# Additions and SiLUs of a gate/up block in a two-layer decoder trunk: placed in the program by hand instead of by a planner

## The chip, the cores and the metric

The kernel runs on one core of one Trainium2 chip. The metric is the device time of one execution in microseconds (us). The time before is the median of three runs. A profile comes from one further execution, which has its own time. TensorE (PE) does the matrix products and loads their weights (PEld), VectorE (DVE) and ScalarE (ACT) do elementwise work, GpSimd (POOL) almost none, and SyncE (SP) issues the loads.

## The reference, cut to what matters

The trunk has one Mamba-2 layer and one attention layer on 256 tokens of width 2048, each followed by a SwiGLU network of width 5632:

```
h = h + mamba2_mixer(rmsnorm(h, ...), ...)
h = h + swiglu(rmsnorm(h, ffn_norm_w[0]), w_gate_up[0], w_down[0])
k, v, cum = shared_kv(h, ...)
h = h + forgetting_attention(rmsnorm(h, ...), k, v, cum, ...)
h = h + swiglu(rmsnorm(h, ffn_norm_w[1]), w_gate_up[1], w_down[1])

def swiglu(h, w_gate_up, w_down):
    g, u = jnp.split(h @ w_gate_up, 2, axis=-1)
    return (jax.nn.silu(g) * u) @ w_down
```

The change touches only the product with `w_gate_up` and the `silu(g) * u` behind it, in both layers.

## The kernel before, in words

All weights are float32. Each weight tile is split into a rounded part `whi` (a cast on ACT, L246) and a remainder `wlo` (a subtraction on DVE, L252), and the activations likewise. A product is then three matmuls of 128x128 by 512 columns: high by high (L491), high by low (L492), low by high (L493). `stream` walks through a list of pieces, each of two 128-row weight slices. It splits a piece some steps (`SPL` = 4) before the piece's matmuls are issued, into rings of four `whi` and four `wlo` buffers, and it issues the loads (L333, 1 MB each, a ring of `RAW` = 3 buffers) behind the splits that free them.

In the gate/up product (`ffn_up`, L616) one block is 512 columns of the gate (left) and 512 of the up half (right), for both tiles of 128 tokens. There are 11 blocks in each layer, 22 in all. The first three quarters of the inner dimension are done plainly: six loads, twelve pieces of 12 matmuls. These accumulate in four PSUM banks of the pool `acc`: left[0], left[1], right[0], right[1]. The last quarter is done in seven products instead of eight, out of sums of the operands (a Strassen-Winograd scheme): the class `Cross`, whose steps run in the order d g a c e b f, six matmuls each (L409 to L411). `split_cross` (L357) splits the operand of each step and forms sums of weights by DVE additions at L364. The products g, b and f are added onto left[0], left[1] and right[0] in PSUM. The product a gets right[1], whose content ACT first copies away (`rest`, L390). The products d, c and e get banks of the pool `mis`.

The steps behind the seven products are those of `early`, `first`, `second` and `third`, generators (tasks) that are put into a queue by `cross_step` behind the steps g, e, b and f:

- `early`: ACT copies d out (L626), DVE forms sg = g + d (L621), ACT applies the gate's SiLU to it (L629). This frees left[0].
- `first`: DVE forms v = e - v and y = c - v (L621).
- `second`: DVE forms y = y + b (L621), which frees left[1]; then ACT applies the SiLU to y (L642).
- `third`: four more additions (L621), two multiplications by the SiLUs (L656), and the transposes of the result on TensorE (L527).

The next block starts with its piece n0, whose six matmuls for token tile 0 go to left[0] and whose next six go to left[1] (before the down projection, where the two alternate by three, the same banks follow). Its pieces are called n0, n1, ... below.

Every engine works through its instructions in the order of the program. Where the tasks' instructions stand in that order is decided by a planner, `Flow`. It keeps a clock for each engine (`at`: E for TensorE, A, V), adds estimated costs to them (1.3 for six matmuls, 1.14 or 1.22 for the subtraction of a split, 0.66 for an addition), and `pump`, called after each six matmuls, issues the next part of the first task in the queue if the task's time and the clocks of A and V are at most 4.0 ahead of E. When a product has its matmuls issued, E is first raised to the planned end of that product's split. When a block's first matmuls are about to be issued, the task of the block before last is finished up to its `EVAC` mark:

```
held.append(b)
if len(held) > 2:
    flow.finish(held.popleft().task, evac=True)
```

Of the kernel before, what the change touches and what calls it, by code (L numbers as in the profile page):

```python
# [38 lines left out]
SPL = 4  # L39
# [45 lines left out]
class Task:  # L85


    def __init__(self, gen, queue, ready=0.0):
        self.gen, self.queue, self.ready = gen, queue, ready
        self.done, self.evac, self.sync, self.on, self.last = False, False, False, None, "E"  # L90


class Flow:
# [7 lines left out]
    def spawn(self, gen, queue=None):  # L101
        q = self.urgent if queue is None else queue
        t = Task(gen, q, max(self.at["E"], self.current.ready if self.current else 0.0))
        q.append(t)
        return t
# [84 lines left out]
class Cross:  # L190
# [6 lines left out]

    ORDER = "dgacebf"

    def __init__(self, left, right, units, x, tasks):  # L200
        self.left, self.right, self.units, self.x, self.tasks = left, right, units, x, tasks
        self.ps, self.rest = {}, None


# [1 line left out]
def kernel(ctx: ExitStack, tc: tile.TileContext, xT_d, x_d, cols_d, rows_d, wdt_d, win_d,  # L206
# [27 lines left out]
    def tok(name):  # L234
        return work.tile([P, NB], F32, tag="tok", name=nm(name))
# [67 lines left out]
        b.units.append(Unit(b, 0, src, width, [list(range(a, min(a + step, nk))) for a in range(0, nk, step)]))  # L303
        blocks.append(b)

    def pair(xs, src_l, src_r, tasks, fills):


        both = []
        for src in (src_l, src_r):  # L310
            b = Block(xs, None, fills if src is src_r else None)
            b.paired = True
            if src is src_r:
                b.stops[1] -= KT
            for kg in range(len(xs) - 1):
                b.units.append(Unit(b, kg, src[kg].rearrange("p (k n) -> p k n", n=NB), NB, [[0, 1], [2, 3]]))
            blocks.append(b)
            both.append(b)
        last = [Unit(None, len(xs) - 1, src[len(xs) - 1].rearrange("p (k n) -> p k n", n=NB), NB, [list(range(KT))])
                for src in (src_l, src_r)]  # L320
        blocks.append(Cross(*both, last, xs[-1], tasks))

    def slot_of(s):
        flow.finish(s.task)
# [57 lines left out]
    def cross_step(x, name, parts):  # L382

        hi, lo, ready = parts
        flow.work("E", 0.0, ready)
        s = slot_of(x.x)
        left, right = x.left.ps, x.right.ps
        if name == "d":
            x.rest = phase.tile([P, NB], F32, tag="c4", name=nm("rest"))
            nc.scalar.copy(out=x.rest, in_=right[1])  # L390
            flow.work("A", 0.48)
        own = {"g": left[0], "b": left[1], "f": right[0]}
        if name in own:
            ps = own[name]
        elif name == "a":
            ps = right[1]
        else:
            ps = bank([P, NB])
        x.ps[name] = ps

        def a_of(part, p):
            if name in "dgb":
                k, t = {"d": (1, 0), "g": (0, 0), "b": (0, 1)}[name]
                return s[:, part, 2 * p + k, t * P:(t + 1) * P]
            return x.x.sums[:, "acef".index(name), part, p, :]

        for p in range(2):
            xh, xl = a_of(0, p), a_of(1, p)
            nc.tensor.matmul(ps, lhsT=xh, rhs=hi[:, p, :], start=p == 0 and name not in own, stop=False)  # L409
            nc.tensor.matmul(ps, lhsT=xh, rhs=lo[:, p, :], start=False, stop=False)  # L410
            nc.tensor.matmul(ps, lhsT=xl, rhs=hi[:, p, :], start=False, stop=p == 1)  # L411
        if name in x.tasks:
            task = spawn(x.tasks[name](x))
            if name == "b":
                x.left.task = task
            if name == "f":
                x.right.task = task
                if x.right.fills is not None:
                    x.right.fills.task = task
        flow.work("E", STEP)  # L420
        flow.pump()

    def stream(pre_load, pre_split):
# [30 lines left out]
        split_to(SPL - 1)  # L454
        held = deque()
        for i, (u, ks) in enumerate(pieces):
            split_to(i + SPL)
            if isinstance(u, Cross):
                cross_step(u, ks, parts[i])
                continue  # L460
            b = u.blk
            nk = KT * len(b.xs)
            hi, lo, ready = parts[i]
            flow.work("E", 0.0, ready)
            if u.width < NB:
                if b.ps is None:
                    b.ps = bank([2 * u.width, T])
                for j, k in enumerate(ks):
                    both = hi[:, j].rearrange("p a n -> p (a n)")
                    s = slot_of(b.xs[k // KT])  # L470
                    nc.tensor.matmul(b.ps, lhsT=both, rhs=s[:, 0, k % KT, :], start=k == 0, stop=False)
                    nc.tensor.matmul(b.ps, lhsT=both, rhs=s[:, 1, k % KT, :], start=False, stop=k == nk - 1)
                flow.work("E", 0.22 * len(ks))
                if ks is u.pieces[-1]:
                    b.task = spawn(b.done(b.ps))
                continue
            if b.ps is None:
# [3 lines that stand above are left out]
                b.ps = [acc.tile([P, u.width], F32, tag="acc", name=nm("acc")) for _ in range(NT)]  # L481
            last = u is b.units[-1] and ks is u.pieces[-1]
            order = [(j, t) for j in range(len(ks)) for t in range(NT)]
            if last or (b.paired and u.kg == 0 and ks[0] == 0):
                order = [(j, t) for t in range(NT) for j in range(len(ks))]
            for n, (j, t) in enumerate(order):
                k = u.kg * KT + ks[j]
                s = slot_of(b.xs[k // KT])
                xh = s[:, 0, k % KT, t * P:(t + 1) * P]
                xl = s[:, 1, k % KT, t * P:(t + 1) * P]  # L490
                nc.tensor.matmul(b.ps[t], lhsT=xh, rhs=hi[:, j, :], start=k == 0, stop=False)  # L491
                nc.tensor.matmul(b.ps[t], lhsT=xh, rhs=lo[:, j, :], start=False, stop=False)  # L492
                nc.tensor.matmul(b.ps[t], lhsT=xl, rhs=hi[:, j, :], start=False, stop=k == b.stops[t])  # L493
                if n % 2 == 1:
                    flow.work("E", STEP)
                    flow.pump()
            if last and not b.paired:
                b.task = spawn(b.done(b.ps))
                if b.fills is not None:
                    b.fills.task = b.task  # L500
# [115 lines left out]
    def ffn_up(xs, r, gu_d):  # L616
        acts = [Slot() for _ in range(NFB)]
        add, sub = ALU.add, ALU.subtract

        def tt(out, in0, in1, op):  # L620
            nc.vector.tensor_tensor(out=out, in0=in0, in1=in1, op=op)  # L621
            return V(0.66)

        def early(x):
            m, d, g = x.ps, tok("d"), tok("sg")
            nc.scalar.copy(out=d, in_=m["d"])  # L626
            yield A(0.48)
            yield tt(g, m["g"], d, add)
            nc.scalar.activation(g, g, AF.Silu, scale=r[0][:, 0:1])  # L629
            yield A(0.6, SILU)  # L630
            x.v, x.g = d, g

        def first(x):
            m, v = x.ps, x.v
            yield tt(v, m["e"], v, sub)
            x.y = tok("y")
            yield tt(x.y, m["c"], v, sub)

        def second(x):
            yield tt(x.y, x.y, x.ps["b"], add)  # L640
            yield EVAC
            nc.scalar.activation(x.y, x.y, AF.Silu, scale=r[0][:, 1:2])  # L642
            yield A(0.6, SILU)

        def third(nb):
            def run(x):
                m, w = x.ps, x.v
                yield tt(w, w, m["a"], add)
                u = tok("u")
                yield tt(u, w, m["c"], sub)  # L650
                yield tt(w, w, m["f"], add)
                yield EVAC
                yield tt(u, u, x.rest, add)
                s = [w, u]
                for t, g in enumerate((x.g, x.y)):
                    nc.vector.scalar_tensor_tensor(out=s[t], in0=s[t], scalar=r[0][:, t:t + 1], in1=g, op0=ALU.mult, op1=ALU.mult)  # L656
                    yield V(0.66)
                yield SYNC
                yield from to_slot(acts[nb], lambda t, f: s[t][:, f * P:(f + 1) * P], None)
            return run  # L660

        for nb in range(NFB):
            pair(xs, gu_d[2 * nb], gu_d[2 * nb + 1], {"g": early, "e": first, "b": second, "f": third(nb)}, acts[nb])
        return acts


# [594 lines left out]
```

## Time and profile before

| | before |
|---|---|
| median of three runs | 2606.91 us (2606.17 to 2607.38) |
| profiled execution, its own time | 2605.81 us |
| its span in the profile | 2604.0 us |
| mean granted TensorE clock | 0.999 of full speed |
| from block to block inside a gate/up stage (transposes at 853.68, 900.11, 946.54 us) | 46.4 us |

The span is the time from the first to the last instruction of the profiled execution; 1.8 us of its time lie around it. Matmul rows overlap: each is shown with 0.39 us although one starts every 0.23 us, so TensorE's gaps are read from the starts. An idle time in brackets names what the instruction waited for.

### The profile page before, as it was taken

What the parts mean: (1) busy time and instruction counts of PE and PEld (TensorE: products, weight loads), DVE (VectorE), ACT (ScalarE), POOL (GpSimd) and SP (SyncE); (2) the same over time, 40 slices, a digit from 0 to 9 for tenths busy, and PEclk for the clock granted to TensorE, in tenths of its full rate; (3) what the DMA queues carried; (4) which work ended last, traced back from release to release, by engine and by line L of the source; (5) the groups of instructions that cost most, each with busy time, mean ns of one, the idle gap of its engine ahead of it and who ended that gap; (6) DMA issues with size and microseconds to landing.
All of it is one profiled execution on the core that took longest, in us unless ns stands there. A gap on an engine that the chain in (4) does not pass through costs nothing.

```text
span 2604.0 us, 29926 instructions
## 1 busy us (share of the span) xinstructions
PE 2541.7 (98%) x11638; PEld 2093.0 (80%) x11638; DVE 1743.0 (67%) x2227; ACT 1326.1 (51%) x1683; POOL 38.4 (1%) x52
## 2 busy tenths in 40 slices
PE   9999999999999999999999999999999999999999
PEld 7888888888877777777888888888877777777887
DVE  6677777654577777777444567775677777776444
ACT  6665565554445454454444556564554544544333
POOL 0000000000000000000000010000000000000000
PEclk9999999999999999999999999999999999999999
DMA  7645455455555545455555555445455554555564
GB/s 273 221 167 178 169 187 184 173 194 189 182 178 186 186 162 200 172 190 183 193 188 188 192 180 195 163 161 179 164 197 188 173 184 162 202 185 180 202 202 144
DMA packets 68319, 481.12 MB, mean 185 GB/s; under 512 B 7600, under 2 KB 8256, under 8 KB 10576
## 3 DMA queue, kind: packets, MB, share of 16 engines
q1 hardware_dynamic: 66672, 468.64, 51.8%
q0 software_dynamic: 1504, 10.57, 1.1%
q8 instruction: 91, 1.49, 0.2%
q14 instruction: 52, 0.43, 0.0%
HBM read 477.00 MB, written 2.18 MB: 184 GB/s over the span
## 4 chain that ended last, share of the span: by engine, by line
PE 92%; DVE 5%; issue 2%; ACT 1%; DMA 0%; SPq 0%; ACTq 0%; DVEq 0%
PE acc L491 27%; PE acc L493 27%; PE acc L492 27%; DVE wlo L252 3%; PE mis L527 1%; DVE y L621 1%; PE mis L912 1%; ACT whi L246 1%; PE acc L410 1%; PE acc L411 1%; PE acc L409 1%; PE mis L411 1%; PE mis L410 1%; PE mis L409 1%; DVE d L621 0%
## 5 line engine op out<-in xcount | busy, mean ns | idle before, releaser
L252 DVE TENSOR_TENSOR wlo<-wraw,whi 128x1024 fp32r<-128x1024 f32 (+1 forms) x851 | 1027.7, 1221 | 622.7 <-ACT whi L246 621.6
L246 ACT CAST whi<-wraw 128x1024 fp32r<-128x1024 f32 (+1 forms) x854 | 883.8, 1049 | 851.4 <-PE acc L493 822.8
L491 PE MATMUL acc<-whi,xT 128*128 128x512 f32 x3040 | 1197.1, 394 | 30.8 <-DVE y L621 30.1
L492 PE MATMUL acc<-wlo,xT 128*128 128x512 f32 x3040 | 1184.9, 390 | 0.8 <-DVE wlo L252 0.8
L493 PE MATMUL acc<-whi,xT 128*128 128x512 f32 x3040 | 1184.6, 390 | 0.0
L491 PEld LDWEIGHTS acc<-whi,xT 128*128 128x128 f32 x3040 | 571.4, 188 | 156.3 <-DVE y L621 39.2
L493 PEld LDWEIGHTS acc<-whi,xT 128*128 128x128 f32 x3040 | 571.1, 188 | 120.0
L492 PEld LDWEIGHTS acc<-wlo,xT 128*128 128x128 f32 x3040 | 571.5, 188 | 117.0 <-DVE wlo L252 1.8
L254 DVE SCALAR_TENSOR_TENSOR wlo<-wraw,cols,whi 128x512 fp32r<-128x512 f32 x192 | 134.6, 748 | 74.3 <-ACT whi L248 73.5
L248 ACT ACTIVATE whi<-wraw,cols 128x512 fp32r<-128x512 f32 x192 | 127.5, 717 | 73.9 <-PE acc L493 68.8
L252 DVE TENSOR_TENSOR xT<-mis,xT 128x512 fp32r<-128x512 f32 x52 | 33.5, 687 | 38.3 <-ACT xT L246 38.3
L246 ACT CAST xT<-mis 128x512 fp32r<-128x512 f32 x52 | 27.9, 589 | 54.5 <-PE mis L527 54.5
L364 DVE TENSOR_TENSOR wraw<-wraw 128x1024 f32<-128x1024 f32 x44 | 53.9, 1226 | 1.5
L364 DVE TENSOR_TENSOR wraw<-wraw,wraw 128x1024 f32<-128x1024 f32 x44 | 53.9, 1224 | 1.5
L410 PE MATMUL acc<-wlo,xT 128*128 128x512 f32 x88 | 37.1, 421 | 16.8 <-DVE wlo L252 16.8
L514 POOL TENSOR_TENSOR rs<-ms,mhalf 128x4 f32<-128x4 f32 (+1 forms) x27 | 29.0, 1075 | 1533.5 <-DVE ms L512 1533.2
L491 PE MATMUL acc<-whi,oT 128*128 128x512 f32 x128 | 50.5, 394 | 0.0
L493 PE MATMUL acc<-whi,oT 128*128 128x512 f32 x128 | 49.9, 390 | 0.0
L492 PE MATMUL acc<-wlo,oT 128*128 128x512 f32 x128 | 49.8, 389 | 0.0
L409 PE MATMUL acc<-whi,xT 128*128 128x512 f32 x88 | 36.9, 419 | 8.9 <-ACT whi L246 8.9
L248 ACT ACTIVATE xT<-mis,cols 128x256 fp32r<-128x256 f32 x64 | 25.5, 475 | 35.1 <-PE mis L527 35.1
L254 DVE SCALAR_TENSOR_TENSOR xT<-mis,cols,xT 128x256 fp32r<-128x256 f32 x64 | 26.8, 478 | 22.3 <-ACT xT L248 22.2
(221 smaller groups left out, 1681.4 us busy)
## 6 DMA issues: line engine op xcount, KB each, us to landing
wraw<-in_gu_dram SPq DMA_DIRECT2D x176, 1024.0 KB, 4.8
wraw<-in_dn_dram SPq DMA_DIRECT2D x88, 1024.0 KB, 4.8
wraw<-in_win_dram SPq DMA_DIRECT2D x78, 1024.0 KB, 4.9
wraw<-in_wout_dram SPq DMA_DIRECT2D x32, 1024.0 KB, 4.8
wraw<-in_wq_dram SPq DMA_DIRECT2D x16, 1024.0 KB, 4.8
wraw<-in_wk_dram SPq DMA_DIRECT2D x16, 1024.0 KB, 4.8
wraw<-in_wv_dram SPq DMA_DIRECT2D x16, 1024.0 KB, 4.8
wraw<-in_wo_dram SPq DMA_DIRECT2D x16, 1024.0 KB, 4.8
```

The lines of the kernel that those rows point to most:

```text
L246: nc.scalar.copy(out=hi, in_=src)
L248: nc.scalar.activation(hi, src, AF.Copy, scale=scal)
L252: nc.vector.tensor_tensor(out=lo, in0=src, in1=hi.bitcast(F32), op=ALU.subtract)
L254: nc.vector.scalar_tensor_tensor(out=lo, in0=src, scalar=scal, in1=hi.bitcast(F32), op0=ALU.mult, op1=ALU.subtract)
L364: nc.vector.tensor_tensor(out=out, in0=in0, in1=in1, op=ALU.add)
L409: nc.tensor.matmul(ps, lhsT=xh, rhs=hi[:, p, :], start=p == 0 and name not in own, stop=False)
L410: nc.tensor.matmul(ps, lhsT=xh, rhs=lo[:, p, :], start=False, stop=False)
L411: nc.tensor.matmul(ps, lhsT=xl, rhs=hi[:, p, :], start=False, stop=p == 1)
L491: nc.tensor.matmul(b.ps[t], lhsT=xh, rhs=hi[:, j, :], start=k == 0, stop=False)
L492: nc.tensor.matmul(b.ps[t], lhsT=xh, rhs=lo[:, j, :], start=False, stop=False)
L493: nc.tensor.matmul(b.ps[t], lhsT=xl, rhs=hi[:, j, :], start=False, stop=k == b.stops[t])
L514: nc.gpsimd.tensor_tensor(out=r, in0=ms, in1=mhalf[:, :width], op=ALU.pow)
```

## The change

The four tasks are replaced by a function `inline`, called by `cross_step` directly behind the matmuls of each step, and one task `rest`, put into the queue behind f. The copy of d stands behind step g, sg = g + d behind step a, v = e - v and y = c - v behind step e, y = y + b behind step b. Both SiLUs move into `rest`, behind its four additions. For step b, `stream` issues the step before the split of the piece four ahead (n1) instead of after it. The left block's task becomes one that is already done, so that the next block forces nothing of the queue.

```diff
-            pair(xs, gu_d[2 * nb], gu_d[2 * nb + 1], {"g": early, "e": first, "b": second, "f": third(nb)}, acts[nb])
+            pair(xs, gu_d[2 * nb], gu_d[2 * nb + 1], inline, rest(nb), acts[nb])
...
@@ cross_step
-        if name in x.tasks:
-            task = spawn(x.tasks[name](x))
-            if name == "b":
-                x.left.task = task
-            if name == "f":
-                x.right.task = task
-                if x.right.fills is not None:
-                    x.right.fills.task = task
+        x.inline(x, name)
+        if name == "b":
+            x.left.task = Task(None, None)
+            x.left.task.done = x.left.task.evac = True
+        if name == "f":
+            x.right.task = x.right.fills.task = spawn(x.rest_of(x))
         flow.work("E", STEP)
         flow.pump()
@@ stream
         for i, (u, ks) in enumerate(pieces):
+            if isinstance(u, Cross) and ks == "b":
+                cross_step(u, ks, parts[i])
+                split_to(i + SPL)
+                continue
             split_to(i + SPL)
             if isinstance(u, Cross):
                 cross_step(u, ks, parts[i])
@@ ffn_up
-        def early(x):
-            m, d, g = x.ps, tok("d"), tok("sg")
-            nc.scalar.copy(out=d, in_=m["d"])
-            yield A(0.48)
-            yield tt(g, m["g"], d, add)
-            nc.scalar.activation(g, g, AF.Silu, scale=r[0][:, 0:1])
-            yield A(0.6, SILU)
-            x.v, x.g = d, g
-
-        def first(x):
-            m, v = x.ps, x.v
-            yield tt(v, m["e"], v, sub)
-            x.y = tok("y")
-            yield tt(x.y, m["c"], v, sub)
-
-        def second(x):
-            yield tt(x.y, x.y, x.ps["b"], add)
-            yield EVAC
-            nc.scalar.activation(x.y, x.y, AF.Silu, scale=r[0][:, 1:2])
-            yield A(0.6, SILU)
-
-        def third(nb):
+        def inline(x, name):
+
+            m = x.ps
+            if name == "g":
+                x.v = tok("d")
+                nc.scalar.copy(out=x.v, in_=m["d"])
+                flow.work("A", 0.48)
+            elif name == "a":
+                x.g = tok("sg")
+                tt(x.g, m["g"], x.v, add)
+                flow.work("V", 0.66)
+            elif name == "e":
+                x.y = tok("y")
+                tt(x.v, m["e"], x.v, sub)
+                tt(x.y, m["c"], x.v, sub)
+                flow.work("V", 1.32)
+            elif name == "b":
+                tt(x.y, x.y, m["b"], add)
+                flow.work("V", 0.66)
+
+        def rest(nb):
             def run(x):
                 m, w = x.ps, x.v
                 yield tt(w, w, m["a"], add)
                 u = tok("u")
                 yield tt(u, w, m["c"], sub)
                 yield tt(w, w, m["f"], add)
                 yield EVAC
                 yield tt(u, u, x.rest, add)
                 s = [w, u]
+                for t, g in enumerate((x.g, x.y)):
+                    nc.scalar.activation(g, g, AF.Silu, scale=r[0][:, t:t + 1])
+                    yield A(0.6, SILU)
                 for t, g in enumerate((x.g, x.y)):
                     nc.vector.scalar_tensor_tensor(out=s[t], in0=s[t], scalar=r[0][:, t:t + 1], in1=g, op0=ALU.mult, op1=ALU.mult)
                     yield V(0.66)
                 yield SYNC
                 yield from to_slot(acts[nb], lambda t, f: s[t][:, f * P:(f + 1) * P], None)
             return run
```

## Rows read from the trace of the kernel before

**Rows 1.** The page's first part: busy time, share of the span, instructions.

```profile
PE 2541.7 (98%) x11638; PEld 2093.0 (80%) x11638; DVE 1743.0 (67%) x2227; ACT 1326.1 (51%) x1683; POOL 38.4 (1%) x52
```

**Rows 2.** Waits of TensorE: who waited for whom, us in total, times, longest.

```profile
PE acc L491 <- DVE y L621: 30.1, 21, 2.1
PE acc L410 <- DVE wlo L252: 16.8, 22, 0.8
PE acc L409 <- ACT whi L246: 8.9, 22, 1.7
```

**Rows 3.** Timeline of one block, TensorE's rows: start, length, [idle before <- releaser].

```profile
919.88 0.39 PE L409 MATMUL mis<-whi,xT 128*128 128x512 f32 x1
...
926.45 0.39 PE L411 MATMUL mis<-whi,xS 128*128 128x512 f32 x1
...
927.18 0.49 PE L409 MATMUL acc<-whi,xT 128*128 128x512 f32 x1 [0.34 <-ACT whi L246]
...
928.44 0.50 PE L410 MATMUL acc<-wlo,xT 128*128 128x512 f32 x1 [0.77 <-DVE wlo L252]
...
932.20 0.39 PE L493 MATMUL acc<-whi,xT 128*128 128x512 f32 x1
...
933.96 0.50 PE L491 MATMUL acc<-whi,xT 128*128 128x512 f32 x1 [1.37 <-DVE y L621]
...
946.38 0.27 PE L527 MATMUL mis<-ident,d 128*128 128x128 f32 x1
```

**Rows 4.** Timeline of the same block, DVE's rows.

```profile
921.21 1.23 DVE L252 TENSOR_TENSOR wlo<-wraw,whi 128x1024 fp32r<-128x1024 f32 x1 [0.24 <-ACT whi L246]
922.47 1.23 DVE L364 TENSOR_TENSOR wraw<-wraw 128x1024 f32<-128x1024 f32 x1
923.61 1.22 DVE L252 TENSOR_TENSOR wlo<-wraw,whi 128x1024 fp32r<-128x1024 f32 x1
924.75 0.68 DVE L621 TENSOR_TENSOR sg<-acc,d 128x512 f32<-128x512 f32 x1
927.16 4.63 DVE L252 TENSOR_TENSOR wlo<-wraw,whi 128x1024 fp32r<-128x1024 f32 x4 [1.73 <-ACT whi L246]
931.71 0.68 DVE L621 TENSOR_TENSOR d<-mis,d 128x512 f32<-128x512 f32 x1
932.42 0.69 DVE L621 TENSOR_TENSOR y<-mis,d 128x512 f32<-128x512 f32 x1
933.22 0.69 DVE L621 TENSOR_TENSOR y<-y,acc 128x512 f32<-128x512 f32 x1
933.82 2.35 DVE L252 TENSOR_TENSOR wlo<-wraw,whi 128x1024 fp32r<-128x1024 f32 x2
...
941.74 0.75 DVE L656 SCALAR_TENSOR_TENSOR u<-u,rs,y 128x512 f32<-128x512 f32 x1
```

**Rows 5.** Timeline of the same block, ACT's rows.

```profile
920.12 1.06 ACT L246 CAST whi<-wraw 128x1024 fp32r<-128x1024 f32 x1 [1.67 <-PE acc L493]
...
922.51 0.58 ACT L626 COPY d<-mis 128x512 f32<-128x512 f32 x1
925.47 0.72 ACT L629 ACTIVATE sg<-sg,rs 128x512 f32<-128x512 f32 x1 [2.38 <-DVE sg L621]
926.10 3.87 ACT L246 CAST whi<-wraw 128x1024 fp32r<-128x1024 f32 x4
931.44 1.99 ACT L246 CAST whi<-wraw 128x1024 fp32r<-128x1024 f32 x2 [1.48 <-DMA wraw<-in_gu_dram]
...
938.47 1.05 ACT L246 CAST whi<-wraw 128x1024 fp32r<-128x1024 f32 x1 [1.70 <-PE acc L493]
```

**Rows 6.** Timeline of the second gate/up stage's first block, ACT's and DVE's rows.

```profile
1886.42 1.28 ACT L629 ACT_TABLE_LOAD   x1 [2.42 <-DVE sg L621]
...
1889.40 4.63 DVE L252 TENSOR_TENSOR wlo<-wraw,whi 128x1024 fp32r<-128x1024 f32 x4 [3.06 <-ACT whi L246]
```

**Rows 7.** The page's DMA issues: count, size, us from issue to landing.

```profile
wraw<-in_gu_dram SPq DMA_DIRECT2D x176, 1024.0 KB, 4.8
```

More of the change, by code (lines that the diff above doesn't have):

```diff
@@ L198, with __init__ @@
     ORDER = "dgacebf"
-    def __init__(self, left, right, units, x, tasks):
-        self.left, self.right, self.units, self.x, self.tasks = left, right, units, x, tasks
+    def __init__(self, left, right, units, x, inline, rest_of):
+        self.left, self.right, self.units, self.x = left, right, units, x
+        self.inline, self.rest_of = inline, rest_of
         self.ps, self.rest = {}, None
@@ L304, in narrow, with pair @@
         blocks.append(b)
-    def pair(xs, src_l, src_r, tasks, fills):
+    def pair(xs, src_l, src_r, inline, rest, fills):
         both = []
@@ L320, in pair @@
                 for src in (src_l, src_r)]
-        blocks.append(Cross(*both, last, xs[-1], tasks))
+        blocks.append(Cross(*both, last, xs[-1], inline, rest))
     def slot_of(s):
```

## The prediction

> **What bounds the kernel now.** I read first the busy shares [rows 1]: TensorE is busy 98% of the span, DVE 67%, ACT 51%. Matmul rows overlap, so this hides gaps, and the second view is TensorE's list of waits [rows 2]. Only three waits come once in each of the 22 gate/up blocks, and all three stand around the seven products: step b's first matmul for its cast, its second for its `wlo`, and a matmul of the next block for the addition of y. Third, I read one block of the timeline, engine by engine.
>
> In TensorE's rows [rows 3] the first five steps d g a c e (30 matmuls, 919.88 to 926.45) run at (926.45 − 919.88)/29 = 0.2266 us each, without a gap. b would follow at 926.68 and starts at 927.18 (0.50 lost); its second matmul would follow at 927.41 and starts at 928.44 (1.03). Then 16 matmuls to 932.20 take 3.76 where 16 × 0.2266 = 3.63 (0.13 of slow restart). The next would start at 932.43, and starts at 933.96 (1.53): it is n0's first matmul into left[1], which y = y + b frees. To the transposes at 946.38 there are 54 matmuls, 12.42 against 12.24 (0.18). Together 0.50 + 1.03 + 0.13 + 1.53 + 0.18 = 3.37 us in each block of 46.4; nothing else in a block stops TensorE.
>
> The cause is in the other two engines' order. ACT [rows 5] copies d out by 923.09 and then has the gate's SiLU next in its queue. That waits 2.38 us for sg = g + d on DVE (924.75 to 925.43), which the program puts behind e's split. The cast of b stands behind the SiLU and starts at 926.10. DVE meanwhile has nothing but `wlo` of b in front and is idle 1.73 us [rows 4]. Then it does four splits in a row (b, f, n0, n1; 1.14 each), and only then v, y and y + b.
>
> **The change part by part.** No instruction is added or taken away; the order changes.
>
> *The SiLU out of ACT's way, sg behind a's step.* Now DVE's queue reads: `wlo` e, `wlo` b, sg, `wlo` f, `wlo` n0, v, y, y + b, `wlo` n1. Up to `wlo` e nothing changes, and its start hangs on TensorE: the cast of c waits for the last piece's buffer (920.12, 0.24 after the cross products start). From there [rows 4, 5]:
> - b's weight sum ends at 922.47 + 1.23 = 923.70. ACT is free since 923.09, and b's ring buffer was g's, read out at about 922.84. ACT's own start behind a DVE end takes 0.04 (925.43 to 925.47), so the cast starts at 923.74, and `wlo` b 1.06 later (as 926.10 to 927.16): 924.80. DVE is ready at 923.61 + 1.14 = 924.75: no idle time is left.
> - sg at 924.80 + 1.14 = 925.94; `wlo` f 0.60 later (as 933.22 to 933.82): 926.54; `wlo` n0 927.68; v 928.82; y 0.71 later, 929.53; y + b 0.80 later, 930.33. TensorE goes on 0.74 after that start (933.22 to 933.96): 931.07 instead of 933.96.
>
> Two parts make this 2.89 us: the idle 1.73, and the split of n1 (1.14), which the new line in `stream` puts behind y + b.
>
> *TensorE on the same clock.* b starts at 926.68; its `wlo` is done at 926.03. f follows at 928.04 and needs `wlo` f at 928.27; it ends at 927.77. n0 follows at 929.40 and needs `wlo` n0 at 929.63; that ends at 928.91. left[0] is free since sg's end at 926.62. n0's second half is due at 930.76 and gets its bank at 931.07. So the first two stalls go, and of the third 0.31 stays, with its restart of 0.18. What is late next is thus the same bank, and DVE's chain from c on sets it. The casts feed this chain in time: f at 924.68, n0 at 925.64 (ACT is free then, and c's buffer since 925.56). Before the down projection the second bank is due 0.68 earlier, but DVE's chain still sets the restart, so the gain there is the same.
>
> *What waits behind the fixed places.* v stands right behind e's matmuls, y + b right behind b's. Were a product late, DVE would stand, and n1's and n2's splits behind it. v comes up at 928.82 while e ends near 926.9, y + b at 930.33 while b ends near 928.3: about 2 us to spare each. `wlo` n1 moves behind y + b, to 930.93 to 932.16; n1 needs it at about 932.8. The cover is 0.7 us; without it each microsecond is TensorE's.
>
> *The SiLUs in `rest`.* They cost 0.72 each as before. By the planner's costs, DVE's clock stands 3 × 1.14 + 3 × 0.66 − 1.3 = 4.1 ahead of TensorE's behind f (splits n0, n1, n2; v, y and y + b; one step), just over the 4.0 allowed, so `rest` starts inside n0: w + a in its middle, the next two additions at its end, the fourth and the first SiLU behind n1, the second SiLU and both multiplications behind n3, the transposes behind n5, one piece later than now. In ACT's queue these SiLUs stand behind casts of n4 and n6 with their operands long there, and ACT waits 1.70 us per piece for TensorE in that stretch [rows 5]: cost nothing; without that cover 1.4 us a block. The last multiplication comes at about 941.4, while the transposes are due near 946.2; now it starts at 941.74 for 946.38 [rows 3, 4].
>
> *Loads.* SP issues as many as before, each behind a split. The load behind f's split goes out at 927.8 instead of 929.5, that behind n1's at 932.2 instead of 931.8. A load lands 4.8 us later [rows 7]: 932.6 and 937.0, for casts that cannot start before about 932.9 and 938.3, when TensorE leaves their buffers at its pace. The load behind e's split keeps its place; its cast was held until 931.44 in this block, and its `wlo` is needed at 935.5, a spare of over 1 us. Cost nothing; if two loads slowed each other by all of a load's length, n2 would wait about 3 us in a block.
>
> *The second stage's first block.* There the SiLU also drags a table load of 1.28 us into the way of b's cast, and DVE idles 3.06 instead of 1.73 [rows 6]. The load moves with the SiLU into ACT's idle time: 1.33 us more, once. The Trainium skill, ScalarE: Activation LUTs (What ACT_TABLE_LOAD costs), counts a drain with the load, about 2.66 us for a switch; by that this block would give about 2.7 us more in place of 1.33 and the sum would grow by 1.3. The row shows the SiLU 0.01 us behind the load's end, so 1.33 stands.
>
> **Sum.** 22 × 2.89 = 63.6, and 1.3: 64.9 us off. The profiled execution's 2605.81 (span 2604.0 and 1.8 around it) becomes 2540.9; the median lies 1.1 above that execution: 2542.0. A difference of 0.2% (5.2 us) is about what a measurement of this kernel can tell from no change. Spacings on DVE can be off by 0.2 us in a chain of nine, 4 to 5 us in all: 2537 to 2548 for this case.
>
> **The rivals.**
> - *The bank wait keeps its length.* b's stalls go, but y + b comes no sooner after n0 than now: only 0.50 + 1.03 + 0.13 = 1.66 a block, 22 × 1.66 + 1.3 = 37.8, 2569. For it: the last bank wait is the longest of the three, and from 921.2 to 934 DVE is idle for those 1.73 us alone. Against it: n1's 1.14 leaves DVE's way by the order of the program alone. A rule of the Trainium skill, Perfetto Trace Analysis (Identifying Performance Opportunities), speaks for it: a gap that repeats can mean too few PSUM buffers, which no reordering mends. The trace agrees in that a bank is what is waited for, but the bank is held by an addition waiting its turn. Chance 8%.
> - *TensorE never stops.* If y + b ends 0.3 sooner than counted, all 3.37 go: 22 × 3.37 + 1.3 = 75.4, 2531.5. Chance 8%.
> - *It does not change what TensorE waits for:* b's cast held by its weight sum, b's `wlo` by sg or by splits. Then 2602 to 2612. It needs b's sum 2.4 us later than 923.70; the row has no such delay. Chance 4%.
> - *Slower: DVE stands at v or y + b.* It decides once the products come more than 2.0 + 2.9 = 4.9 us later than counted against DVE's queue; at 6 us late each block loses 1.1 us, 2607 + 24 = 2631. b's operands are ready 0.6 us ahead of b, so nothing in the rows makes it late. Chance 3%.
>
> My forecast holds 74%; the remaining 3% lie between it and the first rival. The range from 2531 to 2558 takes in the forecast, TensorE that never stops, and DVE chains up to 0.7 us longer per block. Faster by over 0.2%: 93%; within 0.2%: 4%; slower: 3%.
>
> **What would show it.** In the profile after: no wait of step b for cast or `wlo`; TensorE's wait for y's addition down from 1.37 to some 0.2 us as listed; DVE without idle time from `wlo` e to y + b, with sg between the splits of b and f; SiLUs without a wait for DVE; 43.5 us from block to block. I am wrong if a new name stands in TensorE's waits (`wlo` of n1, a transpose, a load), or if the bank wait is still over 1 us.

## The result and the profile after

| | before | after |
|---|---|---|
| median | 2607.14 us (4 runs, 2606.17 to 2610.39) | 2543.02 us (4 runs, 2542.06 to 2543.43) |
| ratio, 95% interval | | 0.9751 [0.9734, 0.9768] |
| span of the profiled execution | 2604.0 us | 2541.7 us |
| from block to block in a gate/up stage | 46.43 us | 43.58 us |

The change makes the kernel 64 us faster. The prediction was 2542.0, in a range from 2531 to 2558. The span and the time from block to block are from one profiled execution of each kernel.

The page after, first part (busy time, share of the span, instructions). The counts are those of [rows 1] and the busy times of DVE and ACT are within 1 us of them: no work went, only waiting. TensorE's busy time fell by 15.2 us too, because a matmul beside a stop shows its whole 0.39 to 0.50 us, and one in a run without stops only the 0.23 up to the next.

```profile
PE 2526.5 (99%) x11638; PEld 2093.4 (82%) x11638; DVE 1742.4 (69%) x2227; ACT 1325.5 (52%) x1683; POOL 37.7 (1%) x52
```

Waits of TensorE after (who for whom, us in total, times, longest), against [rows 2]:

```profile
PE acc L494 <- DVE y L624: 6.8, 22, 0.9
PE acc L494 <- ACT whi L247: 2.2, 2, 1.5
PE mis L1187 <- POOL ident masks.py:199: 1.4, 1, 1.4
PE acc L495 <- DVE wlo L253: 1.0, 2, 0.8
```

Step b's two waits are gone in all 22 blocks. The wait for y's addition is left, 22 times, 6.8 us instead of 30.1. The waits for casts and `wlo` of L494 and L495 lie in the first 15 us of the kernel, where the first loads come in. The change does not touch them.

One block of the timeline after. DVE's rows, against [rows 4]:

```profile
910.89 1.23 DVE L253 TENSOR_TENSOR wlo<-wraw,whi 128x1024 fp32r<-128x1024 f32 x1 [0.24 <-ACT whi L247]
912.15 1.23 DVE L365 TENSOR_TENSOR wraw<-wraw 128x1024 f32<-128x1024 f32 x1
913.29 2.50 DVE L253 TENSOR_TENSOR wlo<-wraw,whi 128x1024 fp32r<-128x1024 f32 x2
915.71 0.68 DVE L624 TENSOR_TENSOR sg<-acc,d 128x512 f32<-128x512 f32 x1
916.31 2.35 DVE L253 TENSOR_TENSOR wlo<-wraw,whi 128x1024 fp32r<-128x1024 f32 x2
918.58 0.68 DVE L624 TENSOR_TENSOR d<-mis,d 128x512 f32<-128x512 f32 x1
919.30 0.69 DVE L624 TENSOR_TENSOR y<-mis,d 128x512 f32<-128x512 f32 x1
920.09 0.69 DVE L624 TENSOR_TENSOR y<-y,acc 128x512 f32<-128x512 f32 x1
920.70 1.22 DVE L253 TENSOR_TENSOR wlo<-wraw,whi 128x1024 fp32r<-128x1024 f32 x1
```

ACT's rows of the same block, against [rows 5]:

```profile
909.80 1.06 ACT L247 CAST whi<-wraw 128x1024 fp32r<-128x1024 f32 x1 [1.67 <-PE acc L496]
...
912.40 0.58 ACT L632 COPY d<-mis 128x512 f32<-128x512 f32 x1
913.48 4.13 ACT L247 CAST whi<-wraw 128x1024 fp32r<-128x1024 f32 x4 [0.51 <-DVE wraw L365]
921.01 2.00 ACT L247 CAST whi<-wraw 128x1024 fp32r<-128x1024 f32 x2 [3.40 <-DMA wraw<-in_gu_dram]
923.50 1.06 ACT L247 CAST whi<-wraw 128x1024 fp32r<-128x1024 f32 x1 [0.49 <-DMA wraw<-in_gu_dram]
924.46 0.72 ACT L658 ACTIVATE sg<-sg,rs 128x512 f32<-128x512 f32 x1
```

TensorE's rows of the same block: the first d, the first b, the last matmul into left[0] and the first into left[1], against [rows 3]:

```profile
909.56 0.39 PE L410 MATMUL mis<-whi,xT 128*128 128x512 f32 x1
...
916.36 0.39 PE L410 MATMUL acc<-whi,xT 128*128 128x512 f32 x1
...
920.21 0.39 PE L496 MATMUL acc<-whi,xT 128*128 128x512 f32 x1
...
920.83 0.50 PE L494 MATMUL acc<-whi,xT 128*128 128x512 f32 x1 [0.24 <-DVE y L624]
```

The reader is to see three things. DVE has no listed idle time from e's `wlo` (913.29) to y + b; between two rows there are at most 0.10 us. The cast of b waits only for its weight sum (L365, ended at 913.38), not for a SiLU; the SiLU runs at 924.46, without a wait. TensorE goes through b and f without a gap and stops once, from 920.44 to 920.83.

The transposes of three blocks, from the chain that ended last, give the time from block to block, 43.58 to 43.60 us (the second and third line are two blocks apart):

```profile
848.93 0.87 PE mis L530 x8
892.51 0.87 PE mis L530 x8
...
979.70 0.88 PE mis L530 x8
```

### The profile page after: what moved, and what is told of

Same layout as the page of the kernel before. It is cut to its first block, busy times and chain, and to the rows that moved or that the text cites. A ratio compares the mean times of both kernels' runs of the same rounds, so it can differ in the third digit from the quotient of the medians.

```text
span 2541.7 us, 29859 instructions
## 1 busy us (share of the span) xinstructions
PE 2526.5 (99%) x11638; PEld 2093.4 (82%) x11638; DVE 1742.4 (69%) x2227; ACT 1325.5 (52%) x1683; POOL 37.7 (1%) x52
## 4 chain that ended last, share of the span: by engine, by line
PE 90%; DVE 7%; ACT 2%; issue 1%; DMA 0%; SPq 0%; ACTq 0%; DVEq 0%
PE acc L494 28%; PE acc L496 28%; PE acc L495 28%; DVE wlo L253 3%; ACT whi L247 2%; PE mis L530 1%; DVE y L624 1%; PE mis L917 1%; DVE wraw L365 1%; DVE sg L624 1%; DVE d L624 1%; PE mis L787 0%; PE mis L923 0%; PE mis L1022 0%; PE mis L852 0%
## 5 line engine op out<-in xcount | busy, mean ns | idle before, releaser
L494 PE MATMUL acc<-whi,xT 128*128 128x512 f32 x3040 | 1196.7, 394 | 9.1 <-DVE y L624 6.8
L495 PE MATMUL acc<-wlo,xT 128*128 128x512 f32 x3040 | 1184.3, 390 | 1.0 <-DVE wlo L253 1.0
L494 PEld LDWEIGHTS acc<-whi,xT 128*128 128x128 f32 x3040 | 571.2, 188 | 134.3 <-DVE y L624 16.1
L495 PEld LDWEIGHTS acc<-wlo,xT 128*128 128x128 f32 x3040 | 571.6, 188 | 116.8 <-DVE wlo L253 1.6
L365 DVE TENSOR_TENSOR wraw<-wraw 128x1024 f32<-128x1024 f32 x44 | 53.9, 1225 | 1.5
L365 DVE TENSOR_TENSOR wraw<-wraw,wraw 128x1024 f32<-128x1024 f32 x44 | 53.9, 1224 | 1.5
L494 PE MATMUL acc<-whi,oT 128*128 128x512 f32 x128 | 50.5, 394 | 0.0
L495 PE MATMUL acc<-wlo,oT 128*128 128x512 f32 x128 | 49.8, 389 | 0.0
L800 DVE SCALAR_TENSOR_TENSOR xf<-mis,cols,xf 128x255 f32<-128x255 f32 (+2 forms) x96 | 39.7, 473 | 2.4 <-ACT xf L794 2.4
```

The costliest lines, as they stand in the source:

```text
L365: nc.vector.tensor_tensor(out=out, in0=in0, in1=in1, op=ALU.add)
L800: nc.vector.scalar_tensor_tensor(out=dst[:, i, s:], in0=pt[half][:, f, :T - s], scalar=col(w + 3 - s), in1=dst[:, i, s:], op0=ALU.mult, op ...
```

## The experiments

Each ratio is against the kernel before on the same chip: 2607.82 us for the first four runs, 2607.28 us for the last three. The changed kernel's 2543.02 us, from which differences are taken, belongs to 2607.14 us before; on the chip of the last three runs it took 2543.70.

**n1's split first.** The changed kernel without its special place for step b:

```diff
-            if isinstance(u, Cross) and ks == "b":
-                cross_step(u, ks, parts[i])
-                split_to(i + SPL)
-                continue
```

> The changed kernel, but the split of n1 stands ahead of b's step again, so that DVE does it between y = c - v and y = y + b. Theory (DVE's queue sets when left[1] comes free): y + b 1.14 us later in each of the 22 blocks, TensorE's wait for it 0.24 + 1.14 = 1.4 us as listed, no wait of step b; 2543.0 + 25.1 = 2568, ratio to before 0.985. Rival (the whole gain came from the SiLU leaving ACT's queue in front of b's cast, the place of n1's split is free): 2543, ratio 0.975.

Measured: 2564.49 us, ratio 0.9832 [0.9816, 0.9849]. The rival, by which the place of n1's split is free, is out. The time is 21.5 us over the changed kernel's instead of 25.1. DVE's rows show why it is less than 22 × 1.14 (the first row, e's and b's splits, serves two runs further on):

```profile
917.83 2.50 DVE L253 TENSOR_TENSOR wlo<-wraw,whi 128x1024 fp32r<-128x1024 f32 x2
...
923.84 0.69 DVE L620 TENSOR_TENSOR y<-mis,d 128x512 f32<-128x512 f32 x1
924.45 1.22 DVE L253 TENSOR_TENSOR wlo<-wraw,whi 128x1024 fp32r<-128x1024 f32 x1
925.58 0.68 DVE L620 TENSOR_TENSOR y<-y,acc 128x512 f32<-128x512 f32 x1
```

Straight behind y, the addition y + b starts 0.80 after it. With the split between, the split starts 0.61 after y and the addition 1.13 after the split: 1.74, so 0.94 more and not 1.14. Twenty-two times 0.94 is 20.7.

**The gate's SiLU early.** The changed kernel with sg and the gate's SiLU behind step g again:

```diff
             if name == "g":
                 x.v = tok("d")
                 nc.scalar.copy(out=x.v, in_=m["d"])
                 flow.work("A", 0.48)
-            elif name == "a":
                 x.g = tok("sg")
                 tt(x.g, m["g"], x.v, add)
                 flow.work("V", 0.66)
+                nc.scalar.activation(x.g, x.g, AF.Silu, scale=r[0][:, 0:1])
+                flow.work("A", 0.6)
...
-                for t, g in enumerate((x.g, x.y)):
-                    nc.scalar.activation(g, g, AF.Silu, scale=r[0][:, t:t + 1])
-                    yield A(0.6, SILU)
+                nc.scalar.activation(x.y, x.y, AF.Silu, scale=r[0][:, 1:2])
+                yield A(0.6, SILU)
```

> The changed kernel, but sg = g + d and the gate's SiLU stand behind step g again, ahead of b's split on DVE and of b's cast on ACT, as in the kernel before; n1's split stays behind y + b. Theory: DVE idle 1.73 us again ahead of b's wlo, TensorE waits at b for the cast (0.34 as listed) and for wlo (0.77) again, y + b 1.75 us later than in the changed kernel; 22 x 1.75 + 1.3 = 39.8 over 2543, so 2583, ratio 0.991. Rival (n1's split alone gave the gain): 2543, ratio 0.975. Rival (the two parts need each other): 2607, ratio 1.000.

Measured: 2582.42 us, ratio 0.9903 [0.9888, 0.9917], as the theory has it. TensorE's waits, and DVE's row with its idle time ahead of b's `wlo`:

```profile
PE acc L411 <- DVE wlo L253: 16.7, 22, 0.8
PE acc L410 <- ACT whi L247: 9.2, 22, 1.7
PE acc L494 <- DVE y L624: 6.5, 21, 0.9
```

```profile
923.01 3.50 DVE L253 TENSOR_TENSOR wlo<-wraw,whi 128x1024 fp32r<-128x1024 f32 x3 [1.73 <-ACT whi L247]
```

DVE's idle 1.73 us are back, and so are the two waits of b as in [rows 2], while the wait for the bank stays as short as in the changed kernel: TensorE now arrives at it as much later as y + b does. So each part of the change is worth something without the other: 25.4 us by the place of n1's split alone (2607.82 to 2582.42), the rest by the SiLU. Here the split is worth its full 22 × 1.14 = 25.1, because in the kernel before it stands in the row of four splits ahead of v [rows 4], and not between y and y + b. The run moves sg and the SiLU together; the next one parts them.

**The SiLUs alone.** The kernel before, planner and all, with only the SiLUs moved (the `EVAC` mark of `second` goes with them; the task now ends where it stood):

```diff
         def early(x):
...
-            nc.scalar.activation(g, g, AF.Silu, scale=r[0][:, 0:1])
-            yield A(0.6, SILU)
             x.v, x.g = d, g
...
         def second(x):
             yield tt(x.y, x.y, x.ps["b"], add)
-            yield EVAC
-            nc.scalar.activation(x.y, x.y, AF.Silu, scale=r[0][:, 1:2])
-            yield A(0.6, SILU)
...
                 s = [w, u]
+                for t, g in enumerate((x.g, x.y)):
+                    nc.scalar.activation(g, g, AF.Silu, scale=r[0][:, t:t + 1])
+                    yield A(0.6, SILU)
```

> The kernel before with its planner and its four tasks; only the two SiLUs are moved behind the four additions of the last task. Theory: the cast of b no longer waits for sg, DVE's order is wlo e, sg, wlo b, wlo f, wlo n0, v, y, wlo n1, y + b as the planner issues it, so y + b comes as in the run with n1's split first: 2568, ratio 0.985, and the fixed places of copy and sg are worth nothing by themselves. Rival (the fixed places are what counts, the planner spoils it): 2600 or more, ratio above 0.997.

Measured: 2559.13 us, ratio 0.9813 [0.9798, 0.9828]. That is 49 us of the 64, and 9 us better than expected; the rival is out. sg stands here where the kernel before had it, and b's two waits are gone all the same: the SiLU made them. The planner's order had been foreseen rightly. Two sizes had not. n1's split costs 0.94 and not 1.14, as above: 22 × 0.2 = 4.4 us. The other is in DVE's rows:

```profile
915.41 1.22 DVE L252 TENSOR_TENSOR wlo<-wraw,whi 128x1024 fp32r<-128x1024 f32 x1
916.54 0.69 DVE L621 TENSOR_TENSOR sg<-acc,d 128x512 f32<-128x512 f32 x1
917.14 3.49 DVE L252 TENSOR_TENSOR wlo<-wraw,whi 128x1024 fp32r<-128x1024 f32 x3
...
923.01 0.68 DVE L621 TENSOR_TENSOR y<-y,acc 128x512 f32<-128x512 f32 x1
```

sg stands between the splits of e and b, while ACT casts b, and the next split starts 0.60 behind it. In the changed kernel the split of b stands there, has to wait for its cast and starts 1.28 after e's instead of 1.14 (913.29 + 2.50 − 1.22 = 914.57). From e's `wlo` to y + b it takes 923.01 − 915.41 = 7.60 here and 925.58 − 917.83 = 7.75 with n1's split first: 0.15 a block, 3.3 us. The two together leave 1.2 us, no more than the 1.4 us between the fastest and the slowest execution of the changed kernel.

**b's bank copied out by ACT.** The changed kernel, with left[1] freed by a copy:

```diff
             elif name == "e":
-                x.y = tok("y")
                 tt(x.v, m["e"], x.v, sub)
-                tt(x.y, m["c"], x.v, sub)
-                flow.work("V", 1.32)
-            elif name == "b":
-                tt(x.y, x.y, m["b"], add)
                 flow.work("V", 0.66)
+            elif name == "b":
+                x.y = tok("y")
+                nc.scalar.copy(out=x.y, in_=m["b"])
+                flow.work("A", 0.48)
...
                 m, w = x.ps, x.v
+                yield tt(x.y, x.y, w, sub)
+                yield tt(x.y, m["c"], x.y, add)
                 yield tt(w, w, m["a"], add)
```

> The changed kernel, but ACT copies b's bank left[1] out behind step b, ahead of n1's cast, and the two operations y = c - v and y = y + b become y = b - v and y = c + y from the copy, at the head of the last task; one ACT copy more per block. Theory (what is left of the bank wait is DVE's queue): left[1] is free about 0.9 us after b ends and 1.8 us before it is needed, TensorE no longer waits for DVE between blocks, 43.05 instead of 43.58 us from block to block, 11 to 12 us off: 2531.5, ratio 0.971. Rival (too few banks or TensorE's own restart): 2543, ratio 0.975. Rival (the copy, waiting for b's product, holds n1's and n2's casts behind it on ACT): 2550 or more, ratio above 0.978.

Measured: 2529.01 us, ratio 0.9699 [0.9684, 0.9713], 14 us below the changed kernel and the fastest version here. TensorE waits for no one in the gate/up stages. Of the 14 us, 22 × (43.58 − 43.06) = 11.4 come from the blocks' own pace, and 1.4 more from the last block of each stage, ahead of the down projection: there the wait for y was 0.91 as listed, not 0.23. The second stage's first block adds 0.4 (its wait was 0.58); the rest is within the spread. ACT's copy (first fence) and the transposes of two blocks running (second, from the chain that ended last):

```profile
914.74 0.59 ACT L643 COPY y<-acc 128x512 f32<-128x512 f32 x1 [1.48 <-PE acc L412]
915.22 1.05 ACT L247 CAST whi<-wraw 128x1024 fp32r<-128x1024 f32 x1
```

```profile
889.33 0.87 PE mis L530 x8
932.39 0.87 PE mis L530 x8
```

The copy waits 1.48 us for b's product and keeps n1's cast back by it, but n1's matmuls come late enough: the second rival is out with the first. 43.06 us from block to block is 186 matmuls at 0.2266 us and 0.87 us of transposes (43.02) to within 0.04.

**One more operation on DVE.** A needless maximum ahead of v, in the changed kernel and in the one with the copy; and the changed kernel itself on the same chip:

```diff
             elif name == "e":
...
+                tt(x.rest, x.rest, x.rest, ALU.max)
                 tt(x.v, m["e"], x.v, sub)
```

> The changed kernel with one needless DVE operation more per block (the maximum of the copied rest with itself, 128x512, in SBUF) ahead of v = e - v, behind n0's split. Theory (DVE's queue up to y + b sets when TensorE goes on, with nothing to spare): all of its 0.60 us shows in each block, TensorE's wait for y as listed 0.84 instead of 0.24; 22 x 0.60 = 13.2 over 2543, so 2556, ratio 0.980. Rival (DVE has slack there and the rest of the bank wait is TensorE's own): 2543, ratio 0.975.

> The kernel in which ACT copies b's bank out, with the same needless DVE operation at the same place. Theory (the copy has taken DVE's queue off TensorE's path; the next thing that hangs on it, n1's split, has over 0.9 us to spare): nothing, 2529, ratio 0.970. Rival (DVE's total work is what costs): 2542, ratio 0.975.

> The changed kernel itself, to be compared on the same chip as the other two: 2543, ratio 0.975 under each theory.

Measured: 2556.27 us, ratio 0.9807 [0.9792, 0.9822], in the changed kernel; 2530.31 us, ratio 0.9705 [0.9689, 0.9722], in the one with the copy; 2543.70 us, ratio 0.9756 [0.9742, 0.9771], for the changed kernel again. So 12.6 us of the 13.2 show where y + b holds the bank (2556.27 against 2543.70). Where it does not, 2530.31 against 2529.01, measured on two chips, cannot be told from no change, and the blocks keep their pace of 43.06. DVE's rows and TensorE's wait with the extra operation in the changed kernel:

```profile
920.22 0.69 DVE L624 TENSOR_TENSOR rest<-rest 128x512 f32<-128x512 f32 x1
920.82 0.68 DVE L624 TENSOR_TENSOR d<-mis,d 128x512 f32<-128x512 f32 x1
```

```profile
PE acc L494 <- DVE y L624: 20.3, 22, 1.5
```

20.3 − 6.8 = 13.5 us more of that one wait: all that is added to DVE's queue there is added to TensorE's wait.

## Why the prediction was right

**The bound.** That TensorE stops only around the seven products, for what the other two engines issue in which order, held: the same instructions in another order took 64 us off.

**DVE's chain.** Predicted from e's `wlo` to y + b: 930.33 − 923.61 = 6.72; measured 920.09 − 913.29 = 6.80. Predicted to TensorE's restart: 931.07 − 923.61 = 7.46; measured 920.83 − 913.29 = 7.54. The 0.08 arises at b's split. It was counted 0.05 behind DVE (924.80 against 924.75) and starts 0.14 behind it, for the most part because its cast starts 0.10 behind the end of the weight sum (913.38 to 913.48) and not 0.04. A block gains 46.43 − 43.58 = 2.85 and not 2.89.

**What is left of the bank wait.** Predicted 0.31 and its restart; measured 0.39 (920.44 to 920.83). That DVE's queue sets it is shown from two sides: a copy on ACT takes it away, and 0.60 us more on DVE lengthen it by 0.6. The first rival had the right place and the wrong size. The Trainium skill, Perfetto Trace Analysis (Identifying Performance Opportunities), takes a repeated gap as a hint of too few PSUM buffers. A bank was what TensorE waited for, yet the gap closed with the banks there are, once the bank was read out sooner. That no reordering mends such a gap was the prediction's own inference, and it is wrong here: the order alone took the wait from 1.53 to 0.39.

**The two parts.** Their sizes were given as 1.73 and 1.14 a block. The experiments that undo one each give 39.4 us for the SiLU's place (2582.42 against 2543.02), as expected, and 21.5 for n1's split, less than 25.1 because the split fills a pause between two additions of which one needs the other's result.

**The cover.** The SiLUs in the last task run without a wait, behind the casts of n4 and n6 as said, and TensorE waits for no transposes. In the times of the block shown before (its first d is at 919.88, here at 909.56: 10.32 later) the casts that waited for the load behind e's split started at 931.33, as before at 931.44; ACT's wait for it is longer (3.40 for 1.48) because ACT is done sooner. The load behind f's split came later than counted: n4's cast started at 933.82, where 932.9 was its earliest. TensorE waited for neither.

**The second stage's first block.** The table load still takes 1.28 us, now off the path:

```profile
1863.86 1.05 ACT L247 CAST whi<-wraw 128x1024 fp32r<-128x1024 f32 x1 [1.43 <-PE acc L496]
1864.93 1.28 ACT L658 ACT_TABLE_LOAD   x1
1866.22 0.72 ACT L658 ACTIVATE sg<-sg,rs 128x512 f32<-128x512 f32 x1
```

Again the SiLU starts 0.01 us behind it. The Trainium skill, ScalarE: Activation LUTs (What ACT_TABLE_LOAD costs), counts a drain beside the load; the trace after shows none, neither behind the load nor ahead of it (the cast before it ends at 1864.91). This block was to gain 1.33 us more than the others. From its first d to the next block's it took 47.75 before (1880.79 to 1928.54), 1.32 over 46.43, and takes 43.97 after (1850.54 to 1894.51), 0.39 over 43.58. So the 1.32 went as predicted, and 0.39 came back, 0.93 net. The 0.39 is DVE's:

```profile
1860.28 0.69 DVE L624 TENSOR_TENSOR y<-mis,d 128x512 f32<-128x512 f32 x1
1861.42 0.69 DVE L624 TENSOR_TENSOR y<-y,acc 128x512 f32<-128x512 f32 x1 [0.45 <-DVE y L624]
```

y + b starts 1.14 behind y here, and not 0.80, well before the table load. Why is open.

**The sum.** 22 × 2.89 + 1.3 = 64.9 was predicted. From the first d of the first stage to the end 63.3 came: 31.29 up to the second stage's first d, 32.05 behind it. The span shrank by 62.3, because the first d of the first stage came 1.04 later in this execution (734.17 to 735.21), ahead of anything that the change touches. In the kernel's first 16 us TensorE waited 1.48 us for a cast, and its clock fell. Before (first fence) and after (second), columns as in the last section:

```profile
12.00:15.50 3.50, 2.88 (x12) 2.17 (x12) 3.38 (x7) 3.36 (x7) 0.00 (x0) 1.00 1.03 425
```

```profile
12.00:15.50 3.50, 3.04 (x7) 2.46 (x8) 3.43 (x7) 3.37 (x6) 0.00 (x0) 0.51 1.03 428
```

The 1.04 goes with this fall: the profiles of two experiments show one there too (0.51 and 0.61), with a first d at 735.24 and 735.97; in the five others, the changed kernel's second among them, the clock stays at 1.00 there and the first d lies from 733.91 to 734.38. So the mechanism and its sizes were right, but that the medians differ by 64.1, within 1 us of the forecast, is in part luck: executions of one kernel lie 1.4 to 4.2 us apart.

**The fixed places** of copy and sg were costed at nothing but the 0.05 above. The run with the SiLUs alone shows that they bring no gain: sg's new place behind b's split is 0.15 us a block worse than the planner's.

## What to carry to other kernels

Where an engine works strictly in order, look at what stands in front of the instruction that the bottleneck waits for, not at busy shares: one SiLU waiting for another engine held back a cast whose operands were there, and 22 such waits were 39 us of 2607. An operation whose result is only needed later belongs behind those that feed the next matmul; an addition that frees a PSUM bank belongs in front of a split that has time. When the bank is held by a long queue, a copy by an engine that is idle there frees it sooner than a better place in the queue: it took the rest of the gap, 14 us, for one more 0.59 us instruction a block.

## What the runs showed of the hardware

Two dependent additions on DVE start 0.71 or 0.80 us apart, while an independent operation follows an addition after 0.60, so that work put between dependent ones costs less than its length (0.94 for 1.14). Where 0.80 is usual it was once 1.14 or 1.15 in four of the traces: in both of the changed kernel in the second stage's first block, in the first stage's first block with the gate's SiLU early, and in its ninth with one more operation on DVE.

TensorE's clock fell in one block of the kernel before, where the table load made the break at b longer. The views by windows, before (first fence) and after (second): stretch and length, busy time (instructions) of PE, PEld, DVE, ACT, POOL, then granted clock, DMA share, GB/s.

```profile
1888.00:1891.00 3.00, 0.81 (x2) 0.48 (x3) 1.60 (x2) 3.00 (x4) 0.00 (x0) 1.00 0.63 268
1891.00:1894.50 3.50, 3.50 (x10) 2.73 (x9) 3.50 (x4) 2.26 (x3) 0.00 (x0) 0.52 0.51 138
```

```profile
1855.00:1858.00 3.00, 3.00 (x15) 2.48 (x14) 2.94 (x4) 2.88 (x4) 0.00 (x0) 1.00 0.44 120
1858.00:1862.00 4.00, 3.58 (x16) 2.63 (x14) 3.51 (x5) 2.16 (x3) 0.00 (x0) 1.00 0.96 379
```

Behind a stretch with two matmuls the granted clock was 0.52, about the 1.2 GHz level, and from 1894.5 on 0.99. It cost nothing in the kernel before: TensorE came to left[1] at 1896.26, when y + b (from 1895.46, and 0.74 as elsewhere) had just freed it. This is the one block of the 22 whose wait for y is missing in [rows 2], and its 1.32 us over the others are what DVE's longer idle time makes (3.06 for 1.73). It is gone after the change. With the gate's SiLU early, where y + b comes sooner behind b, the clock fell in the same block (0.50 from 1878.1 to 1881.4), and that block took 2.16 us over the others (47.46 against 45.30): 0.8 more than DVE's idle time makes, which is then the clock's. In the other 21 blocks of the kernel before the breaks left the clock at 1.00 (0.999 over the span).
